# Sums of gate weights added up in DRAM by accumulating DMAs in place of subtractions on VectorE

## The chip, the cores and the metric

One core of a Trainium2 chip runs the whole program. The metric is device time in microseconds: three runs of the kernel before took 1419.89, 1419.94 and 1420.02 us, so the median is 1419.94 us. Everything is float32. Products on TensorE are made from operands split into a high part (fp32r) and a low remainder, so that each product is three matmuls (high by high, high by low, low by high).

## The reference

The input is 1024 tokens by 1024 channels. One wide projection of the normalised input feeds two branches and their gates; the part that the change touches is the gates.

```python
xn = rmsnorm(x, norm1_g[layer])
u = xn @ w_in[layer].astype(f32)
...
q_sb, k_sb, v_sb, f_raw, i_hg, q_hg, g_hg, gate_sb, gate_hg = jnp.split(u, list(c), axis=-1)
...
o_sb = stick_breaking_attention(split_heads(q_sb, SB_HEADS), split_heads(k_sb, SB_HEADS),
                                split_heads(v_sb, SB_HEADS))
...
o_hg = hgrn2_chunkwise(split_heads(jax.nn.silu(q_hg), HG_HEADS), split_heads(k_hg, HG_HEADS),
                       split_heads(i_hg, HG_HEADS), split_heads(log_f, HG_HEADS))
...
o_hg = merge_heads(o_hg) * jax.nn.silu(g_hg)
...
g_a = jax.nn.sigmoid(gate_sb + bg[:D_MODEL])
g_b = jax.nn.sigmoid(gate_hg + bg[D_MODEL:])
merged = g_a * (o_sb @ w_o_sb[layer].astype(f32)) + g_b * (o_hg @ w_o_hg[layer].astype(f32))
h = x.astype(f32) + merged @ w_out[layer].astype(f32)
hn = rmsnorm(h, norm2_g[layer])
a = jnp.square(jax.nn.relu(hn @ w_ff1[layer].astype(f32)))
h = h + a @ w_ff2[layer].astype(f32)
```

## The kernel before

**Stages.** Norm and first projections (up to about 95 us of the profile), attention over 8 heads and 8 query blocks each (64 items, up to about 330 us), the gated recurrence for 4 heads with the first gate products and the attention's output projection as filler (up to about 590 us), the rest of the gates (up to about 718 us), the output projection (up to about 800 us), the MLP.

**Gates.** The four 512x512 quarters of a gate's product (two halves of the tokens by two gates, each over two halves of the channels) are computed by a Strassen-Winograd scheme with seven products instead of eight. For this each gate column block `cb` needs plain weights and four signed sums of weight quarters. There are ten column blocks: `cb` 0 to 7 hold the two merge gates, `cb` 8 and 9 the recurrence's own gate `g_hg`. Class `RawUnit` (L1333) makes two of the seven products ahead, from plain weights and one sum; class `GatePair` (L1530) makes the others from four sums. Both load the plain 128-column strips of `w_in` and form the sums with `sub` (L1291, a VectorE tensor_tensor), then split them.

**Fill work.** `Stream` `st` holds projection jobs (`proj_jobs`, `raw_job`, `i_job`, `sb_job`, listed from L1512) and puts some of their matmuls between the steps of attention and recurrence. When a job starts, `prefetch` splits the weights of the next job and loads those of the one after, so loads run one or two jobs ahead. `RawUnit.split_t` is done in three parts at steps 4, 6 and 8 of the job before (L548).

**Queues.** Weight loads go out on SyncE's queue (SP) in the order of the code (`load`, L135). Accumulating DMAs, and some stores, go out on GpSimd's queue (POOL), where memsets and small norm operations stand too. A DMA that reads or adds to what an earlier one wrote waits, on its issuing engine, for that one's landing; GpSimd's DMAs use eight completion semaphores in turn, so that each also waits for the landing of the eighth before it. An engine runs its instructions in a fixed order, so whatever stands behind a waiting instruction waits too.

**Around the change.** `out_weight_sums` (L1312) already adds up the sums of the output projection's weights in DRAM (`tw`): 16 plain copies and then 16 additions of 256 KB, one in every second item of attention (L2382). At the end of attention GpSimd sums the two halves of the last head's output in place (`osb`, L911); SyncE then stores it (`od`, L922, called at L2404). Behind that store on SyncE's queue stand the loads of the next weights, `wf3` and `wq3` (L136).

Of the kernel before, what the change touches and what calls it, by code (L numbers as in the profile page):

```python
# [39 lines left out]
def kernel(  # L40
# [462 lines left out]
    class Stream:  # L503
# [36 lines left out]
        def step(self):  # L540

            if self.gen is None:
                if self.pos >= len(self.jobs):
                    return False
                self.steps = 0
                self._start()
            self.steps += 1
            if self.owed_t and self.steps in (4, 6, 8):  # L548
                self.owed_t.split_t(hg_level[0] or turn_lo[0], self.steps // 2 - 1)
                if self.steps == 8:  # L550
                    self.owed_t = None
# [760 lines left out]
    def out_weight_sums():  # L1312
# [3 lines left out]
        for op, ways in ((ALU.bypass, plain), (ALU.add, summed)):  # L1316
            for i, src in ways:
                for r in range(4):
                    rs = slice(r * P, (r + 1) * P)
                    after(nc.gpsimd.dma_start(tw[i][rs], src[rs], accum_op=op), lastsel[0])  # L1320
                    yield

    def gate_bias(which, cb):
        return prm[:, BG + which * KT + cb : BG + which * KT + cb + 1]

# [7 lines left out]
    class RawUnit(Unit):  # L1333


        late = True
        turned = 0

        def __init__(self, cb):
            dmas = [  # L1340
                [(0, P, W_IN[:, gate_cols(w, cb)].rearrange("(k p) c -> p k c", p=P))]
                for w in range(2)
            ]
            super().__init__(f"wga{cb}", dmas)
            if cb < KT:
                self.roomy = (1,)

        def split(self):
            if self.hl is not None:
                return  # L1350
            self.load()
            ra, rb = self.raw
# [3 lines left out]
            hi_lo(h, l, ra)  # L1356
            self.hl = [(h, l)]

        def split_t(self, behind=None, upto=3):
            ra, rb = self.raw  # L1360
            while self.turned < upto:
                self.turned += 1
                if self.turned == 1:
                    after(sub(rb, ra, rb), behind)
                elif self.turned == 2:
                    after(sub(rb[:, 512:], rb[:, 512:], rb[:, 0:512]), behind)
                else:
                    t = slot(f"{self.name}t", F32R)
                    self.hl.append((t[:, 0:512], t[:, 512:]))
                    after(hi_lo(*self.hl[1], rb[:, 512:]), behind)  # L1370

    raw_units = [RawUnit(cb) for cb in range(NG)]

    def raw_job(cb):
        u = raw_units[cb]

        def steps_of(ps, wt, w0, half_, k0, start):
            wh, wl = u.hl[wt]
            for k in range(4):
                c = (w0 + k) * P  # L1380
                xh, xl = xn.mov(k0 + k, half_)
                three(
                    ps, wh[:, c : c + P], wl[:, c : c + P], xh, xl, start and k == 0, k == 3, True
                )
                if k % 2 == 1:
                    yield

        def body():
            p1, p14, g1 = (half(f"{n}_{cb}") for n in ("p1", "p14", "g1"))
            ps, p4 = bank(f"pga{cb}"), bank(f"pgq{cb}")  # L1390
# [12 lines left out]
            hi_behind[0] = None  # L1403
            yield from steps_of(p4, 1, 0, 1, 4, True)
            add(p14, p1, p4)
            if cb == 3 or cb == KT - 1:
                whole_input(1, int(cb == KT - 1))
            nc.gpsimd.dma_start(pd[cb][:, 1, :], p14)
# [27 lines left out]
    def sum_forms():  # L1436


        raw = whole
        def split(m, kp, src):  # L1440
            forms[m, kp] = tuple(slot(f"gs{n}{m}{kp}", F32R) for n in "hl")
            hi_lo(*forms[m, kp], src)

        for j in range(2):
            whole_input(0, j)
        yield from range(WAIT)
        s1, s2 = {}, {}
        for kp in range(2):
            s1[kp] = slot(f"gs1{kp}")
            ins = add(s1[kp], raw[1, 0, kp], raw[1, 1, kp])  # L1450
            if kp == 0:
                after(ins, hg_sum[0])
            yield
        for kp in range(2):
            split(5, kp, s1[kp])
            yield
        for kp in range(2):
            s2[kp] = slot(f"gs2{kp}")
            sub(s2[kp], s1[kp], raw[0, 0, kp])
            yield  # L1460
            split(6, kp, s2[kp])
            yield
        gates_in[0].load()
        gates_in[0].load_sums()
        for kp in range(2):
            s3 = slot(f"gs3{kp}")
            sub(s3, raw[0, 0, kp], raw[1, 0, kp])
            split(7, kp, s3)
            yield
        gates_in[0].split()  # L1470
        for kp in range(2):
            s4 = slot(f"gs4{kp}")
            sub(s4, raw[0, 1, kp], s2[kp])
            split(3, kp, s4)
            yield
        gates_in[1].load()
# [35 lines left out]
    for h in range(1, NHS):  # L1512
        j_qk[h] = proj_jobs([qk_item(h)], xn)
        if h == 2:
            raw_job(KT)
        if h == 4:
            q_job(0)
    f_job(0)
    f_job(1)
    q_job(1)  # L1520
# [9 lines left out]
    class GatePair:  # L1530
# [3 lines left out]
        def load(self):  # L1534
            cb = self.cb
            self.raw = [
                wpool.tile([P, 1024], F32, tag="raw", name=f"wg{cb}r{i}") for i in range(2)
            ]
            for i, s_, which in ((0, 0, 0), (0, 1, 1), (1, 1, 1)):
                load(  # L1540
                    self.raw[i][:, s_ * 512 : (s_ + 1) * 512].rearrange("p (k c) -> p k c", k=4),
                    W_IN[i * 512 : (i + 1) * 512, gate_cols(which, cb)].rearrange(
                        "(k p) c -> p k c", p=P
                    ),
                )
# [18 lines left out]
        def split(self, behind=None):  # L1564
            cb = self.cb
            r0, r1 = self.raw
            s0, s1 = slice(0, 512), slice(512, 1024)
            first = behind if self is gates_in[3] else None
# [93 lines left out]

        def y3(self):
            self.product(3, self.Y, False)
            add(self.u2, self.u2, self.Y)
            self.gate(self.u2, 1)

        def early_half(self):
# [740 lines left out]
    for h in range(NHG + 1):  # L2409
# [4 lines left out]
        while going:  # L2414
            going = False
            for g in (lev, tail):
# [9 lines left out]
            st.finish(max(j_f[h + 1], j_q[h + 1]))  # L2426
    st.finish(j_sb[2])
    for _ in side[0]:
        pass
    gates()  # L2430

# [97 lines left out]
```

## Time and profile before

| what | us |
|---|---|
| median of three runs | 1419.94 |
| span of the profiled execution | 1418.4 |
| what lies around the span, by these two | 1.5 |
| TensorE (PE) busy | 1408.7 |
| VectorE (DVE) busy | 1086.9 |
| ScalarE (ACT) busy | 684.9 |
| GpSimd (POOL) busy | 147.3 |

The page gives each engine's busy time, a picture of the span in 40 slices, the DMA queues, the chain of work that ended last and the costliest groups of instructions. In a timeline's row stand start, duration, engine, line, operation, tiles (out<-in) and, in brackets, how long the engine sat idle before it and what ended that. SPq and ACTq are the sequencers that issue DMAs. "f32 x1" or "x1" at the end counts merged instructions.

### The profile page before, as it was taken

The page shows a single profiled execution, that of the slowest core. Times are in us where ns is not written, and L with a number is a line of the kernel's source. Part 1 is how long each engine was busy: PE and PEld are TensorE (multiplying, and loading weights), DVE is VectorE, ACT ScalarE, POOL GpSimd, SP SyncE. Part 2 cuts the span into 40 slices and gives each one's busy share as a digit, 9 for nine tenths or more (in the row PEclk, how much of TensorE's full clock was granted, in tenths as well). Part 3 has the DMA queues.
Part 4 walks back from the last instruction along what each step waited for, and adds up shares of the span by engine and source line. Part 5 has one row for each costly group of instructions (what it writes and reads, how often), then busy time and mean ns, then how long its engine had stood idle before and what let it go on. Part 6 is the DMA issues. An engine that isn't in the chain of part 4 may idle for free.

```text
span 1418.4 us, 18800 instructions
## 1 busy us (share of the span) xinstructions
PE 1408.7 (99%) x6848; PEld 1183.6 (83%) x6848; DVE 1086.9 (77%) x1493; ACT 684.9 (48%) x1183; POOL 147.3 (10%) x341
## 2 busy tenths in 40 slices
PE   9999999999999999999999999999999999999998
PEld 7888888888888888888888888888888888888886
DVE  7679988988567888887788897676666657668765
ACT  6356676664243554433344764445444443534343
POOL 3012223210011031000000300000000000000042
PEclk9999999999999999999999999999999999999999
DMA  7124445535135685364585514444446974776725
GB/s 238 30 67 127 105 100 98 107 77 157 59 74 171 224 225 178 126 215 156 162 298 193 186 54 169 163 163 143 137 145 239 353 265 149 279 273 238 278 94 188
DMA packets 163173, 237.72 MB, mean 168 GB/s; under 512 B 26332, under 2 KB 93448, under 8 KB 163080
## 3 DMA queue, kind: packets, MB, share of 16 engines
q1 hardware_dynamic: 146056, 190.37, 40.0%
q0 software_dynamic: 11584, 34.61, 10.0%
q10 hardware_dynamic: 5440, 11.54, 2.3%
q8 instruction: 54, 0.88, 0.3%
q14 instruction: 39, 0.32, 0.1%
HBM read 168.32 MB, written 66.06 MB: 165 GB/s over the span
## 4 chain that ended last, share of the span: by engine, by line
PE 98%; DVE 1%; ACT 0%; POOL 0%; DMA 0%; issue 0%; POOLq 0%; SPq 0%; DVEq 0%
PE pm L128 21%; PE pX L128 9%; PE pW L128 6%; PE pY L128 6%; PE pjqk L128 6%; PE pga L128 4%; PE gX L128 4%; PE gY L128 4%; PE pjf L128 3%; PE pjq L128 3%; PE pys L128 3%; PE pji L128 3%; PE pyh L128 3%; PE pjv L128 3%; PE po L128 3%; PE z L128 2%
## 5 line engine op out<-in xcount | busy, mean ns | idle before, releaser
L156 ACT CAST whid<-w 128x1024 fp32r<-128x1024 f32 x30 | 31.6, 1053 | 154.5 <-PE pm L128 87.4
L831 DVE TENSOR_TENSOR_SCAN rm<-rm,bits 128x511 f32<-128x511 f32 (+7 forms) x72 | 87.3, 1219 | 16.4 <-ACT rm L809 16.4
L128 PE MATMUL pm<-wlod,sh 128*128 128x512 f32 x240 | 93.5, 390 | 0.0
L128 PE MATMUL pm<-whid,sl 128*128 128x512 f32 x240 | 93.4, 389 | 0.0
L128 PE MATMUL pm<-whid,sh 128*128 128x512 f32 x240 | 93.4, 389 | 0.0
L128 PE MATMUL pm<-tl,sh 128*128 128x512 f32 (+1 forms) x210 | 81.3, 387 | 0.0
L128 PE MATMUL pm<-th,sl 128*128 128x512 f32 (+1 forms) x210 | 81.3, 387 | 0.0
L128 PE MATMUL pm<-th,sh 128*128 128x512 f32 (+1 forms) x210 | 81.3, 387 | 0.0
L161 DVE TENSOR_TENSOR wlod<-w,whid 128x1024 fp32r<-128x1024 f32 x30 | 36.7, 1222 | 55.3 <-ACT whid L156 55.3
L161 DVE TENSOR_TENSOR sl<-sa,sh 128x1024 fp32r<-128x1024 f32 x56 | 68.2, 1218 | 0.0
L156 ACT CAST wTh<-pw 128x512 fp32r<-128x512 f32 (+2 forms) x96 | 43.8, 485 | 41.9 <-PE pw L131 41.0
L2148 POOL TENSOR_SCALAR fss<-fss 128x1 f32<-128x1 f32 x8 | 4.5, 561 | 562.0 <-ACT fsc L2143 561.5
L156 ACT CAST sh<-sa 128x1024 fp32r<-128x1024 f32 x56 | 57.2, 1046 | 7.2 <-DMA sa<-ad 7.2
L161 DVE TENSOR_TENSOR wTl<-pw,wTh 128x512 fp32r<-128x512 f32 (+2 forms) x96 | 49.9, 546 | 4.6 <-ACT wTh L156 4.4
L128 PEld LDWEIGHTS pm<-wlod,sh 128*128 128x128 f32 x240 | 45.1, 188 | 10.0 <-DVE wlod L161 0.4
L128 PEld LDWEIGHTS pm<-whid,sh 128*128 128x128 f32 x240 | 45.0, 188 | 9.5
L128 PEld LDWEIGHTS pm<-whid,sl 128*128 128x128 f32 x240 | 45.0, 188 | 9.1
L169 DVE TENSOR_TENSOR bt<-bt,rm 128x511 f32<-128x511 f32 (+7 forms) x72 | 48.9, 684 | 3.5
L809 ACT ACTIVATE rm<-z 128x511 f32<-128x511 f32 (+4 forms) x96 | 48.0, 500 | 5.5 <-PE z L128 2.8
L128 PE MATMUL pX<-sqh,t1l 128*128 128x512 f32 x128 | 49.9, 390 | 0.0
L128 PE MATMUL pX<-sql,t1h 128*128 128x512 f32 x128 | 49.9, 390 | 0.0
L128 PE MATMUL pX<-sqh,t1h 128*128 128x512 f32 x128 | 49.8, 389 | 0.0
(932 smaller groups left out, 4434.8 us busy)
## 6 DMA issues: line engine op xcount, KB each, us to landing
w<-in_w_ff_dram SPq DMA_DIRECT2D x72, 512.0 KB, 4.8
sa<-ad SPq DMA_DIRECT2D x52, 512.0 KB, 6.4
ad<-a SPq DMA_DIRECT2D x32, 256.0 KB, 4.3
ad<-s SPq DMA_DIRECT2D x16, 512.0 KB, 3.3
tw<-in_w_out_dram POOLq DMA_DIRECT2D x24, 256.0 KB, 4.6
pr<-pd SPq DMA_DIRECT2D x10, 512.0 KB, 6.0
x<-in_x_dram SPq DMA_DIRECT2D x8, 512.0 KB, 7.8
xnl<-xnh POOLq DMA_DIRECT2D x8, 512.0 KB, 6.5
```

The source lines that it names most:

```text
L128: return pe(nc.tensor.matmul(*a, **k))
L156: hi_last[0] = after(in_turn("act", nc.scalar.copy(dst, src)), hi_behind[0])
L161: nc.vector.tensor_tensor(out=dst, in0=src, in1=hi.bitcast(F32), op=ALU.subtract),
L169: return nc.vector.tensor_tensor(out=out, in0=a, in1=b, op=ALU.mult)
L809: nc.scalar.activation(rm[:, s0 + c0 - 1 : s0 + m - 1], z[:, c0:m], AF.Sigmoid, scale=-0.125)
L831: sc = nc.vector.tensor_tensor_scan(out=rr, data0=rr, data1=bits[:, 1024 - nk + a : 1024 - nk + b][:, ::-1], initial=rm[:, b : b + 1] if i ...
L2148: nc.gpsimd.tensor_scalar(out=ssq, in0=ssq, scalar1=1.0 / D, scalar2=EPS, op0=ALU.mult, op1=ALU.add)
```

## The change

The sums of the gate weights are no longer formed on VectorE. They are added up in DRAM, once and for all columns, into `tg1` to `tg4` (1 and 3 stacked as `tg13`), by 43 DMAs on GpSimd's queue: 32 on blocks of 128 rows by 1024 columns for the merge gates (8 of them copy an earlier sum), and 11 on 512 rows of pairs of 128-column strips for `g_hg` (`gh_sum`), which move runs of 512 bytes. Each moves 512 KB. The 32 DMAs for the output weights follow in the same generator. It is stepped in every second item of attention (32 steps) and at every step of the recurrence (43 steps). The signs of the scheme are turned so that every sum is an addition, and in five places where products or input sums are combined `add` and `sub` change over. `RawUnit` now loads one plain strip and one sum (256 KB instead of 512 KB) and splits the sum in one part; `GatePair` loads three sums and one plain quarter (1 MB instead of 768 KB) and has no subtraction left. The jobs `raw_job(KT)` and `q_job(0)` change places.

```diff
@@ class Stream, step()
-            if self.owed_t and self.steps in (4, 6, 8):
-                self.owed_t.split_t(hg_level[0] or turn_lo[0], self.steps // 2 - 1)
-                if self.steps == 8:
-                    self.owed_t = None
+            if self.owed_t and self.steps == 6:
+                self.owed_t.split_t(hg_level[0] or turn_lo[0])
+                self.owed_t = None
@@ new
+    def gate_weight_sums():
...
+        def add_up(dst, src, op):
+            after(nc.gpsimd.dma_start(dst, src, accum_op=op), lastsel[0])
+
+        def gh_sum(t, *terms):
+            for j, (i, which) in enumerate(terms):
+                add_up(gh_of(tg[t]), gh(i, which), ALU.add if j else ALU.bypass)
+                yield
...
+        def steps(t, op, src):
+            for r in range(4):
+                add_up(part(t, r), part(src, r) if type(src) is int else block(*src, r), op)
+                yield
...
+        yield from both(
+            gh_sum(4, (0, 0), (0, 1), (1, 0), (1, 1)), steps(1, ALU.bypass, (0, 0))
+        )
+        yield from steps(1, ALU.add, (0, 1))
+        yield from steps(2, ALU.bypass, 1)
+        yield from steps(2, ALU.add, (1, 1))
+        yield from steps(4, ALU.bypass, 2)
+        yield from steps(4, ALU.add, (1, 0))
+        yield from steps(3, ALU.bypass, (0, 1))
+        yield from both(gh_sum(2, (0, 0), (0, 1), (1, 1)), steps(3, ALU.add, (1, 1)))
+        outs = out_weight_sums()
+        yield from both(gh_sum(1, (0, 0), (0, 1)), (next(outs) for _ in range(2)))
+        yield from both(gh_sum(3, (0, 1), (1, 1)), (next(outs) for _ in range(2)))
+        yield from outs
...
@@ class RawUnit
-                if self.turned == 1:
-                    after(sub(rb, ra, rb), behind)
-                elif self.turned == 2:
-                    after(sub(rb[:, 512:], rb[:, 512:], rb[:, 0:512]), behind)
...
+            load(t[:, 0:512].rearrange("p (k c) -> p k c", k=4), gate_sum(tg[4], self.cb))
@@ class GatePair, load() and split()
+            load(r0, gate_sum(tg13, cb))
+            load(r1[:, 0:4], gate_sum(tg[2], cb))
+            load(r1[:, 4:8], W_IN[512:, gate_cols(1, cb)].rearrange("(k p) c -> p k c", p=P))
...
-            after(sub(r0[:, s0], r0[:, s1], r0[:, s0]), first)
-            sub(r1[:, s0], r1[:, s1], r0[:, s0])
...
-            sub(r0[:, s1], r1[:, s1], r0[:, s1])
@@ signs
-            ins = add(s1[kp], raw[1, 0, kp], raw[1, 1, kp])
+            ins = sub(s1[kp], raw[1, 0, kp], raw[1, 1, kp])
...
-            self.y_sum = add(p1, p1, self.Y)
-            add(p1, p1, self.X)
+            self.y_sum = sub(p1, self.Y, p1)
+            sub(p1, p1, self.X)
@@ jobs
         if h == 2:
+            q_job(0)
+        if h == 4:
             raw_job(KT)
-        if h == 4:
-            q_job(0)
@@ attention, then recurrence
-    wsums = out_weight_sums()
+    wsums = gate_weight_sums()
...
-        if i % 2 == 1:
+        if i % 2 == 0:
             next(wsums, None)
...
                 if next(g, StopIteration) is not StopIteration:
                     going = True
+                    next(wsums, None)
```

The instruction order on GpSimd's queue, where attention ends and the recurrence begins. `tw` are the sums of the output weights, `pd9` the store of the last product made ahead in attention, `osb7` the summing of the last head's output, `hss0` and `hn0` the first norm of the recurrence. Before:

```order
L867 MEMSET wTh7_2_4_3586 128x128
L867 MEMSET wTl7_2_4_3587 128x128
L1320 DMA tw_131<-tw_131 128x512
L1408 DMA pd9_112<-p14_9_3649 128x512
L911 DMA osb7_3545<-osb7_3545 64x1024
L265 TENSOR_SCALAR hss0_0_4326<-hss0_0_4326 128x4
L269 TENSOR_TENSOR hn0_0_y_4339<-hss0_0_4326,expo_91 128x4
```

The same place now, from the first DMA behind the last memsets of attention; `512x2x128` marks the strips of `gh_sum`, `128x1024` the blocks:

```order
L1336 DMA tg2_143<-in_w_in_dram 512x2x128
L1336 DMA tg13_142<-in_w_in_dram 128x1024 x2
L1336 DMA tg2_143<-in_w_in_dram 512x2x128
L1336 DMA tg13_142<-in_w_in_dram 128x1024 x2
L1336 DMA tg2_143<-in_w_in_dram 512x2x128
L1336 DMA tg13_142<-in_w_in_dram 512x2x128
L1319 DMA tw_131<-in_w_out_dram 128x512
L1465 DMA pd9_112<-p14_9_3649 128x512
L1319 DMA tw_131<-in_w_out_dram 128x512
L1336 DMA tg13_142<-in_w_in_dram 512x2x128 x2
L1319 DMA tw_131<-in_w_out_dram 128x512 x2
L910 DMA osb7_3545<-osb7_3545 64x1024
```

Behind `osb7` follow one more strip DMA, 28 for `tw`, and only then `hss0`. So the 43 steps written into the recurrence stand together on GpSimd's queue, ahead of the recurrence's first norm, and 14 of them stand ahead of `osb7`. The second strip DMA of `tg2` adds to what the first wrote, and the third to the second, so each waits for the landing of the one before it; so does the second strip DMA of `tg1` in `tg13`.

SyncE's queue at the same place. `wir` are the weights of the recurrence's values, `od3` the store of `osb7`, `wf3` and `wq3` the next projections' weights, `wga0` those of the first `RawUnit` of the recurrence. Before:

```order
L136 DMA wir3_3691<-in_w_in_dram 128x2x512
L922 DMA od3_3547<-osb7_3545 64x1024
L136 DMA wf3r0_3743<-in_w_in_dram 128x8x128
L136 DMA wq3r0_4276<-in_w_in_dram 128x8x128
L136 DMA wga0r0_4282<-in_w_in_dram 128x8x128
L136 DMA wga0r1_4284<-in_w_in_dram 128x8x128
```

Now:

```order
L136 DMA wir3_3690<-in_w_in_dram 128x2x512
L921 DMA od3_3547<-osb7_3545 64x1024
L136 DMA wf3r0_3742<-in_w_in_dram 128x8x128
L136 DMA wq3r0_4291<-in_w_in_dram 128x8x128
L136 DMA wga0r0_4297<-in_w_in_dram 128x8x128
L136 DMA wga0r1_4299<-tg4_144 128x4x128
```

Nothing has moved here but the source of `wga0`'s second load: the store of `osb7` still stands ahead of the loads of `wf3` and `wq3`.

More of the change, by code (lines that the diff above doesn't have):

```diff
@@ L1321, in out_weight_sums, with gh, gh_of, block @@
                     yield
+    TGW = NG * P
+    tg13 = dram("tg13", [1024, TGW])
+    tg = {1: tg13[0:512], 3: tg13[512:1024]}
+    tg.update({i: dram(f"tg{i}", [512, TGW]) for i in (2, 4)})
+    def gate_weight_sums():
+        def gh(i, which):
+            rows = W_IN[i * 512 : (i + 1) * 512, C_GH : C_GH + HGW]
+            return rows.rearrange("k (c w p) -> w k c p", w=2, p=P)[which]
+        def gh_of(t):
+            return t[:, KT * P :].rearrange("k (c p) -> k c p", p=P)
+        def add_up(dst, src, op):
[4 more added lines that the diff above has]
+                yield
+        def block(i, which, r):
+            c0 = (C_GA, C_GB)[which]
+            return W_IN[i * 512 + r * P : i * 512 + (r + 1) * P, c0 : c0 + D]
+        def part(t, r):
+            return tg[t][r * P : (r + 1) * P, 0:D]
+        def steps(t, op, src):
+            for r in range(4):
+                add_up(part(t, r), part(src, r) if type(src) is int else block(*src, r), op)
+                yield
+        def both(a, b):
+            for _ in a:
+                yield
+                if next(b, StopIteration) is not StopIteration:
+                    yield
+            yield from b
+        yield from both(
[12 more added lines that the diff above has]
+        yield from outs
+    def gate_sum(t, cb):
+        return t[:, cb * P : (cb + 1) * P].rearrange("(k p) c -> p k c", p=P)
     def gate_bias(which, cb):
@@ L1336, with load @@
         late = True
-        turned = 0
+        turned = False
         def __init__(self, cb):
[L1340 to L1346, printed above, removed]
+            src = W_IN[:, gate_cols(0, cb)].rearrange("(k p) c -> p k c", p=P)
+            super().__init__(f"wga{cb}", [[(0, P, src)]])
+            self.cb = cb
+        def load(self):
+            if self.raw is not None:
+                return
+            super().load()
+            if self.cb < KT:
+                t = slot(f"{self.name}r1")
+            else:
+                t = wpool.tile([P, 1024], F32, tag="raw", name=f"{self.name}r1")
+            load(t[:, 0:512].rearrange("p (k c) -> p k c", k=4), gate_sum(tg[4], self.cb))
+            self.raw.append(t)
         def split(self):
@@ L1351, in split @@
             self.load()
-            ra, rb = self.raw
             h, l = (
@@ L1355, in split, with split_t @@
             )
-            hi_lo(h, l, ra)
+            hi_lo(h, l, self.raw[0])
             self.hl = [(h, l)]
[L1359 to L1362, printed above, removed]
-                if self.turned == 1:
-                    after(sub(rb, ra, rb), behind)
-                elif self.turned == 2:
-                    after(sub(rb[:, 512:], rb[:, 512:], rb[:, 0:512]), behind)
[L1367 to L1370, printed above, removed]
+        def split_t(self, behind=None):
+            if not self.turned:
+                self.turned = True
+                t = slot(f"{self.name}t", F32R)
+                self.hl.append((t[:, 0:512], t[:, 512:]))
+                after(hi_lo(*self.hl[1], self.raw[1][:, 0:512]), behind)
     raw_units = [RawUnit(cb) for cb in range(NG)]
@@ L1389, in body @@
             p1, p14, g1 = (half(f"{n}_{cb}") for n in ("p1", "p14", "g1"))
-            ps, p4 = bank(f"pga{cb}"), bank(f"pgq{cb}")
+            ps, pq = bank(f"pga{cb}"), bank(f"pgq{cb}")
             if 6 <= cb < KT:
@@ L1403, in body @@
             hi_behind[0] = None
-            yield from steps_of(p4, 1, 0, 1, 4, True)
-            add(p14, p1, p4)
+            yield from steps_of(pq, 1, 0, 1, 4, True)
+            add(p14, p1, pq)
             if cb == 3 or cb == KT - 1:
@@ L1472, in sum_forms @@
             s4 = slot(f"gs4{kp}")
-            sub(s4, raw[0, 1, kp], s2[kp])
+            add(s4, raw[0, 1, kp], s2[kp])
             split(3, kp, s4)
@@ L1538, in load @@
             ]
[L1539 to L1545, printed above, removed]
+            r0, r1 = (r.rearrange("p (k c) -> p k c", k=8) for r in self.raw)
+            load(r0, gate_sum(tg13, cb))
+            load(r1[:, 0:4], gate_sum(tg[2], cb))
+            load(r1[:, 4:8], W_IN[512:, gate_cols(1, cb)].rearrange("(k p) c -> p k c", p=P))
             if cb >= KT:
@@ L1567, in split @@
             s0, s1 = slice(0, 512), slice(512, 1024)
-            first = behind if self is gates_in[3] else None
-            after(sub(r0[:, s0], r0[:, s1], r0[:, s0]), first)
-            sub(r1[:, s0], r1[:, s1], r0[:, s0])
             h, l = (
@@ L1664, in y3 @@
             self.product(3, self.Y, False)
-            add(self.u2, self.u2, self.Y)
+            sub(self.u2, self.Y, self.u2)
             self.gate(self.u2, 1)
@@ L2428 @@
     for _ in side[0]:
+        pass
+    for _ in wsums:
         pass
```

## The prediction

> **What bounds the kernel now.** I read the page from the top, then the table of waits, then windows.
>
> ```profile
> span 1418.4 us, 18800 instructions
> PE 1408.7 (99%) x6848; PEld 1183.6 (83%) x6848; DVE 1086.9 (77%) x1493; ACT 684.9 (48%) x1183; POOL 147.3 (10%) x341
> PE 98%; DVE 1%; ACT 0%; POOL 0%; DMA 0%; issue 0%; POOLq 0%; SPq 0%; DVEq 0%
> ```
>
> TensorE is busy for all but 9.7 us, and 98% of the chain that ended last is PE. A busy PE is not PE at its peak, so I looked at what PE waits for (total, times, longest), and at how many matmuls it gets through in stages of different kinds (columns: window, its length, then busy time and count of PE, PEld, DVE, ACT, POOL, then clock, DMA share, GB/s).
>
> ```profile
> PE warm L128 <- POOL ident masks.py:199: 2.2, 1, 2.2
> PE po L128 <- DVE wTl L161: 0.3, 1, 0.3
> 600.00:700.00 100.00, 100.00 (x443) 82.81 (x442) 82.67 (x120) 32.53 (x44) 8.13 (x15) 1.00 0.54 174
> 1000.00:1100.00 100.00, 100.00 (x443) 82.81 (x442) 68.49 (x96) 46.37 (x67) 0.00 (x0) 1.00 0.51 180
> ```
>
> The largest wait is 2.2 us at the start; after it the largest is 0.3. The gate stage (600 to 700), where the subtractions stand, runs 443 matmuls per 100 us, the MLP (1000 to 1100) the same 443, both at granted clock 1.00, although VectorE is busy 82.67 us in the one and 68.49 in the other. So no wait on VectorE hides in the matmul rate, and PE has no idle time in which a late operand could be made good: what PE once waits is lost in full.
>
> **What goes.** Each `RawUnit` had two subtractions, each `GatePair` three; ten of each make 50.
>
> ```profile
> L1292 DVE TENSOR_TENSOR wga7r<-wga7r,wga7r 128x1024 f32<-128x1024 f32 x1 | 1.2, 1233 | 0.0
> L1292 DVE TENSOR_TENSOR wg3r<-wg3r,wg3r 128x512 f32<-128x512 f32 x2 | 1.4, 690 | 0.0
> ```
>
> One of the five is 1024 wide, four 512: 10 x 1.23 + 40 x 0.69 = 39.9 us of VectorE. PE's instructions are the same in kind and number, so their saving is worth what PE waits for VectorE: 0.3 us, as above. I take 0. The turned signs swap `add` for `sub` on one shape, 0. The parts of `split_t` merged into one: same work, 0. The two swapped jobs have the same matmuls, 0.
>
> **Loads.** A `GatePair` loads 256 KB more, a `RawUnit` 256 KB less. Ten times 256 KB over the gate stage (about 590 to 718 us) are 2.6 MB in 128 us, 20 GB/s on top of 174, with DMA engines 0.54 busy: hidden. Were that cover gone, 256 KB would cost a unit what its load lasts, 5.0 us in the row of `wg0` below. The first DMAs for `g_hg` stand ahead of attention's first copies of q on POOL's queue. One issue costs 0.53 us in a plain row, and 1.05 us in an adding one (rows below); the far end for a strip DMA with its runs of 512 bytes, which the trace does not show on this queue, is eight times that, 8.4 us.
>
> ```profile
> 91.00 0.53 POOL L698 DMA_DIRECT2D QL<-QL  x1 [0.71 <-DVE QL L161]
> 99.87 0.39 PE L128 MATMUL z<-KS,QL 128*128 128x512 f32 x1
> QL<-QL POOLq DMA_DIRECT2D x16, 128.0 KB, 2.2
> L1433 POOL DMA_DIRECT2D xnl<-xnh x8 | 7.5, 1047 | 5.7 <-PE pjq L128 4.8 <-PE pga L128 0.8
> wg0r<-in_w_in_dram SPq DMA_DIRECT2D x3, 256.0 KB, 5.0
> ```
>
> (The third row and the last are groups of DMA issues: KB each, us from issue to landing; so are those further on. The fourth is a group of instructions: busy, mean ns of one, idle before.) The copy lands at 93.2 and is read at 99.87: 6.7 us of room, so the far end costs 1.7 us, the near one nothing; I take 0.
>
> **The DMAs added.** 32 of 75 are stepped through attention, one per two items (about 7 us apart), so they keep up. But the order of POOL's queue shows that the 43 written into the recurrence stand in one block right behind attention's last memsets, 14 of them ahead of `osb7`, the sum of the last head's output. The block starts where today's last addition for `tw` is issued, at 306.9.
>
> ```profile
> 306.88 0.81 POOL L1320 DMA_DIRECT2D tw<-tw  x1
> 323.19 0.59 POOL L1408 DMA_DIRECT2D pd<-p  x1 [15.50 <-DVE p L1289]
> 328.16 0.85 POOL L911 DMA_DIRECT2D osb<-osb  x1 [4.38 <-ACT osb L907]
> 333.61 0.51 SPq L922 DMA_DIRECT2D od<-osb  x1
> 336.36 0.37 SPq L136 DMA_DIRECT2D wf3r<-in_w_in_dram  x1
> 340.23 1.05 ACT L156 CAST wf3h<-wf3r 128x1024 fp32r<-128x1024 f32 x1 [0.55 <-DMA wf3r<-in_w_in_dram]
> 343.53 0.62 ACT L1067 COPY ksl<-k 128x512 f32<-128x512 f32 x1
> 346.60 0.60 PE L128 MATMUL sl<-q,ksl 128*128 128x128 f32 x4
> ```
>
> Read from the bottom: PE's `sl` at 346.60 needs ACT's copy `ksl`, done at 344.15, so 2.45 us of room. On ACT that copy stands behind the CAST of `wf3`, which starts when its load has landed, 3.87 us after the issue (340.23 - 336.36). That load stands on SP's queue behind the store `od`, which waits until `osb` has landed (`od` is issued at 333.61, so at about 333.5). If `osb` lands late, the CAST starts 0.1 + 0.51 + 3.87 = 4.5 us after the landing, and PE stalls for landing + 4.5 - 340.23 - 2.45 = **landing - 338.2**. Today's room is 4.7 us. Behind the waiting `od` stand the loads of `wf3`, `wq3` and `wga0`, behind the CAST all of ACT's work.
>
> When does `osb` land? Each adding DMA on strips waits, at issue, for the one before it on the same sums, and each DMA for the landing of the eighth before it, so POOL cannot run far ahead of the landings. Two stretches show accumulations alone on POOL's queue (one `osb` with two and three `tw` sums).
>
> ```profile
> 266.90:274.60 7.70, 7.70 (x42) 6.44 (x41) 6.24 (x11) 5.02 (x12) 2.35 (x10) 1.00 0.77 103
> 298.20:306.90 8.70, 8.70 (x55) 7.74 (x55) 7.96 (x12) 4.48 (x13) 3.59 (x16) 1.00 0.82 122
> xnl<-xnh POOLq DMA_DIRECT2D x8, 512.0 KB, 6.5
> hd<-h POOLq DMA_DIRECT2D x8, 512.0 KB, 3.3
> GB/s 238 30 67 127 105 100 98 107 77 157 59 74 171 224 225 178 126 215 156 162 298 193 186 54 169 163 163 143 137 145 239 353 265 149 279 273 238 278 94 188
> ```
>
> They moved 103 and 122 GB/s with the DMA engines 0.77 and 0.82 busy, mean 112; 512 KB accumulated land in 6.5 us, 512 KB stored plainly in 3.3. Ahead of `osb`, with itself, stand four block additions, two of the three strip DMAs of `tg2` and one of `tg1`, which all add: 7 x 0.524 + 0.262 = 3.93 MB, at 112 GB/s 35 us. So the additions alone end at 306.9 + 35 = **342**. Plain traffic in the same time: three strip copies, one block copy (the last step that attention takes), four of `tw`, the `pd` store, four loads `wir` and some ACT stores, about 6 MB; at 353 GB/s, the highest slice of the page, 17 us. Were nothing of it hidden, `osb` would land at **359**. The windows leave a fifth of the DMA time free, 7 of 35 us; that hides 7 of the 17, and the other 10 come on top: 306.9 + 35 + 10 = **352**. The stall is 352 - 338.2 = 13.8 us, the ends 3.8 and 20.8.
>
> Later on the queue stand 29 more DMAs ahead of the recurrence's first norm. By the same prices (17 additions, 4.7 MB, 42 us; 12 plain, 3.1 MB, 9 us) they end at 352 + 51 = 403.
>
> ```profile
> 403.84 0.19 POOL L265 TENSOR_SCALAR hss<-hss 128x4 f32<-128x4 f32 x1 [74.83 <-ACT hon L1247]
> L136 SPq DMA_DIRECT2D wout2r<-tw x2: 377/377/377, 712.6 to 715.4; - x2
> wir<-in_w_in_dram SPq DMA_DIRECT2D x4, 512.0 KB, 3.9
> wga0r<-in_w_in_dram SPq DMA_DIRECT2D x2, 512.0 KB, 4.6
> ```
>
> That norm stands at 403.84 today and moves back with the stall to 417, so 14 us of room: 0. The first `tw` block is read at 712.6: 0.
>
> **Sum.** Span 1418.4 + 13.8 = 1432.2, and the 1.5 us by which the median (1419.94) is above this execution's span give **1433.7 us**. Its own range: 1419.9 + 3.8 = 1423.7 to 1419.9 + 20.8 = 1440.7. The strips' short runs are a term that I left at the blocks' price: loads in runs of 512 bytes (`wga0`, 4.6 us) last 1.2 times those in longer runs (`wir`, 3.9), so three adding strips (14 us) would cost 2.8 more: 1443.5, which I round up to 1445.
>
> **Rivals.**
> (1) *The queue keeps up.* If additions move like plain stores, the 10 MB ahead of and with `osb` take 28 us at 353 GB/s, end at 335, under 338.2, and nothing stalls: 1419.9 (within 0.2%, or 2.8 us, about what a measurement of this kernel can tell from no change). For it: the additions in the two windows never had more than four in a row, so their queue may not have been full. Against it: `xnl`, 512 KB in 6.5 us. Chance 0.20.
> The Trainium skill bears on this rival ("DMA: Bandwidth & Descriptors", section "Anatomy of one DMA — SWDGE (gpsimd) path"): it fits a GpSimd DMA by some 2.0 us and its bytes over 436 GB/s, without a word on accumulation. By that, an estimate, 512 KB would land in 3.2 us; the trace agrees for the plain `hd` (3.3) and not for the accumulating `xnl` (6.5). By the fit the 3.93 MB of additions would take 9 us behind a full queue, and the sum would be 1419.9.
> (2) *The strips are much dearer.* If runs of 512 bytes make an addition four times as slow, three of them cost 3 x 14 us more, and the time is about 1475. For it: an accumulation reads and writes each run, and no row shows one on short runs. Against it: the 1.2 of the loads. Chance of over 1445: 0.10.
> (3) *Faster: VectorE's relief in attention.* Two `RawUnit`s are split there, in a stretch where VectorE is busy 92%:
>
> ```profile
> 100.00:200.00 100.00, 100.00 (x577) 86.46 (x576) 91.52 (x127) 69.86 (x158) 23.29 (x86) 1.00 0.48 114
> ```
>
> Their subtractions, 2 x (1.23 + 0.69) = 3.8 us, would pass to PE if VectorE set the pace there: 1416.1. It decides if PE's instructions last longer for VectorE's sake without a wait in the records. Against it: PE is busy 100.00 of 100, and of PE's waits only 0.3 us name `wTl`. It also needs a block that stalls nothing. Chance 0.03.
>
> **How the numbers follow.** The forecast has 0.67, rival (2) 0.10, both slower by over 0.2%: 0.77. Rival (1) is the 0.20 within 0.2%, rival (3) the 0.03 faster. The range takes in rival (1) and the strips' bound, 1419 to 1445, and leaves out (2) and (3), 0.13.
>
> **What would show it.** In the changed kernel's waits of PE a new row for `sl` of some 14 us near 347, released by ACT's `ksl`, whose chain goes back to the CAST of `wf3`, its load, `od` and `osb`; on SP's queue `od` at about 352 instead of 333.61; POOL's `osb` issued at 345 to 350; nothing new from 600 on. If `od` is issued before 338, rival (1) holds. If the strip DMAs of `tg2` land far over 6.5 us after issue, it is (2). If PE waits somewhere else, above all before 306 or behind 400, my step of the queue's order was wrong: a stall in attention for the first 32 DMAs, or `hss0` late behind the 28 for `tw`.

## The result, and the profile after

The changed kernel takes 1459.86 us (median of four runs, 1458.12 to 1460.68) against 1419.91 for the kernel before: ratio 1.028, 95% interval 1.0265 to 1.0295. It is 40 us slower. The direction is the one forecast, but the size is three times the 13.8 us forecast, and it lies outside the range, which ended at 1445.

The first lines of the changed kernel's page, and the shares of the chain that ended last:

```profile
span 1456.3 us, 18801 instructions
PE 1413.7 (97%) x6848; PEld 1186.7 (81%) x6848; DVE 1054.3 (72%) x1443; ACT 683.8 (47%) x1183; POOL 187.9 (13%) x384
PE 92%; DMA 3%; DVE 2%; issue 1%; ACT 1%; POOL 1%; POOLq 0%; SPq 0%; ACTq 0%; DVEq 0%
```

The span is 37.9 us longer. PE's time outside its busy time went from 9.7 to 42.6 us (1456.3 - 1413.7), so 32.9 us are waits; the other 5.0 are in PE's busy time, although its instructions are the same. The chain, once 98% PE, now runs through DMAs for 3% of the span. What PE waits for (total, times, longest):

```profile
PE sl L128 <- ACT ksl L1066: 25.5, 1, 25.5
PE sd L128 <- ACT sd_h L156: 5.3, 2, 4.8
PE warm L128 <- POOL ident masks.py:199: 2.2, 1, 2.2
PE po L128 <- DVE wTl L161: 0.9, 1, 0.9
```

Two new waits make the loss. The large one is at the `sl` that the prediction named. The other, at `sd`, was not forecast. Windows of the gate stage and of the MLP, as before (columns as in the prediction):

```profile
600.00:700.00 100.00, 100.00 (x443) 82.81 (x442) 71.99 (x100) 35.09 (x48) 6.47 (x12) 1.00 0.56 181
1000.00:1100.00 100.00, 100.00 (x443) 82.81 (x442) 69.44 (x96) 46.88 (x67) 0.00 (x0) 1.00 0.43 150
```

VectorE has fallen from 82.67 to 71.99 us in 100, and PE still runs 443 matmuls: nothing gained and nothing lost there. The place of the loss, from the timelines of GpSimd, SyncE, ScalarE and PE, in order of the chain:

```profile
312.21 22.70 SPq L136 DMA_DIRECT2D wir<-in_w_in_dram  x4
332.22 1.04 ACT L156 CAST wih<-wir 128x1024 fp32r<-128x1024 f32 x1 [8.49 <-DMA tg<-in_w_in_dram]
336.48 0.79 PE L128 MATMUL sd<-sd_h,ones 128*128 128x512 f32 x1 [4.75 <-ACT sd_h L156]
342.82 1.95 POOL L910 DMA_DIRECT2D osb<-osb  x1
351.61 0.51 SPq L921 DMA_DIRECT2D od<-osb  x1
351.72 1.05 PE L128 MATMUL sl<-q,ksl 128*128 128x128 f32 x8
352.29 0.46 SPq L136 DMA_DIRECT2D wf3r<-in_w_in_dram  x1
352.84 1.22 SPq L136 DMA_DIRECT2D wq3r<-in_w_in_dram  x1
370.45 1.04 ACT L156 CAST wf3h<-wf3r 128x1024 fp32r<-128x1024 f32 x1 [20.67 <-DMA wf3r<-in_w_in_dram]
380.78 1.04 ACT L156 CAST wq3h<-wq3r 128x1024 fp32r<-128x1024 f32 x1 [9.29 <-DMA wq3r<-in_w_in_dram]
382.40 2.08 PE L128 MATMUL sl<-q,ksl 128*128 128x128 f32 x8 [25.54 <-ACT ksl L1066]
441.09 0.19 POOL L265 TENSOR_SCALAR hss<-hss 128x4 f32<-128x4 f32 x1 [49.29 <-ACT hon L1246]
```

`od` went out at 351.61 (forecast: about 352), so the last head's sum landed when it was expected to. But the loads behind it did not take 3.87 us: `wf3` was split 18.2 us after its issue (370.45 - 352.29) and `wq3` 27.9 us after (380.78 - 352.84). The first row and the second show the same earlier: the second of the four `wir` loads reaches ScalarE at 332.22, where it did at 324.19 before. (The bracket of that row names a `tg` DMA, which this CAST does not read; that the load of `wir` ended the wait is inferred from what the CAST reads.) The recurrence's first norm (441.09) still waits for ScalarE, not for the 28 sums ahead of it. The DMA queues from 352.2 to 380.8 (q0 is GpSimd's, q1 SyncE's; share of 16 engines' time; then KB and us to landing), and two rows of the same view from 308 to 351.6:

```profile
q0 software_dynamic: 3087, 5.67, 89.9%
q1 hardware_dynamic: 2160, 1.31, 17.3%
wq3r<-in_w_in_dram SPq DMA_DIRECT2D x1, 512.0 KB, 27.9
...
tg<-in_w_in_dram POOLq DMA_DIRECT2D x12, 512.0 KB, 9.5
wir<-in_w_in_dram SPq DMA_DIRECT2D x4, 512.0 KB, 10.1
```

The DMA engines were full, nine tenths of it with sums, and SyncE's queue needed 2160 packets for 1.31 MB, most of them 512 bytes long. In the kernel before, the `sl` ahead of the one that now waits, and the load of `wq3` (DMA view from 307 to 340), were:

```profile
341.61 1.05 PE L128 MATMUL sl<-q,ksl 128*128 128x128 f32 x8
wq3r<-in_w_in_dram SPq DMA_DIRECT2D x1, 512.0 KB, 5.1
```

### The profile page after: what moved, and what is told of

The parts are those of the page before. It is cut to its first block, busy times and chain, and to the rows that moved or that the text cites. A ratio compares the mean times of both kernels' runs of the same rounds, so it can differ in the third digit from the quotient of the medians.

```text
span 1456.3 us, 18801 instructions
## 1 busy us (share of the span) xinstructions
PE 1413.7 (97%) x6848; PEld 1186.7 (81%) x6848; DVE 1054.3 (72%) x1443; ACT 683.8 (47%) x1183; POOL 187.9 (13%) x384
## 4 chain that ended last, share of the span: by engine, by line
PE 92%; DMA 3%; DVE 2%; issue 1%; ACT 1%; POOL 1%; POOLq 0%; SPq 0%; ACTq 0%; DVEq 0%
PE pm L128 21%; PE pX L128 9%; PE pW L128 6%; PE pY L128 6%; PE pjqk L128 5%; PE gX L128 4%; PE gY L128 4%; PE pga L128 3%; PE pys L128 3%; PE pyh L128 3%; PE pjv L128 3%; PE pjq L128 3%; PE pji L128 3%; PE pjf L128 2%; PE po L128 2%; PE pwX L128 2%
## 5 line engine op out<-in xcount | busy, mean ns | idle before, releaser
L156 ACT CAST wTh<-pw 128x128 fp32r<-128x128 f32 (+3 forms) x96 | 44.0, 486 | 42.7 <-PE pw L131 39.0
L128 PE MATMUL sl<-q,ksl 128*128 128x128 f32 x192 | 26.6, 282 | 25.5 <-ACT ksl L1066 25.5
```

Of the source, the lines that this page charges most:

```text
L128: return pe(nc.tensor.matmul(*a, **k))
L156: hi_last[0] = after(in_turn("act", nc.scalar.copy(dst, src)), hi_behind[0])
```

## The experiments

Three theories stood against each other: (1) the loads meet the queue of sums and are slowed by it; (2) only the order on SyncE's queue matters (a store that waits, loads behind it), as the prediction had it; (3) the extra DMA traffic costs its time wherever it stands. Times are medians; the kernel before was measured beside them at 1419.97 to 1420.07.

**Without the late sums.** The 43 DMAs are left out; the loads that would read their sums take plain weights of the same shape.

```diff
-                    next(wsums, None)
...
-    for _ in wsums:
-        pass
...
-            load(r0, gate_sum(tg13, cb))
+            load(r0, W_IN[:, gate_cols(0, cb)].rearrange("(k p) c -> p k c", p=P))
```

> The 43 sums that stand behind attention are left out; the loads that would read them take plain weight columns of the same shape, so the gates and the output projection are computed from wrong weights. All else of the change stays: 32 sums in attention, no subtractions, turned signs, swapped jobs. If the loss comes from the block of 43 alone, as I think: the waits near 336 and 382 are gone, and what is left is the 0.5 us that the trace of the change shows at 167, so 1420.4 us (1419.5 to 1421). If a part of the loss comes from the other edits (the 32 sums in attention, the larger loads of the gate stage), it stays here: 1423 or more. If VectorE's relief were worth something that the block hid, under 1417.

Measured: 1421.42 us, ratio 1.0011 (1.0001 to 1.002). That is a little over the expected range. Of the 40 us, 38.4 belong to the 43 DMAs. The rest is one wait, in the waits of PE:

```profile
PE po L128 <- DVE wTl L161: 1.8, 1, 1.8
```

**The jobs back in their places**, on top of that; the first products then take a plain strip in place of `tg4`.

```diff
         if h == 2:
-            q_job(0)
+            raw_job(KT)
         if h == 4:
-            raw_job(KT)
+            q_job(0)
```

> As the run without the 43 late sums (1421.42), with the jobs q_job(0) and raw_job(KT) back in their old places; the first products ahead then take a plain weight strip in place of the sum tg4, which would not be ready, so they too are computed from wrong weights. If the 1.5 us left in that run, a wait of PE for wTl near 168, come from the swapped jobs: 1419.9 to 1420.3. If they come from the 32 sums in attention or the loads: 1421 to 1422 still.

Measured: 1420.18 us, ratio 1.0001 (0.9992 to 1.001), and the row above is back at 0.3 us. So the remaining 1.2 us come with the swapped jobs (or with `tg4` as their source, which changed in the same step), and the rest of the change, the 50 subtractions and the 32 sums in attention among it, moves nothing.

**The store on GpSimd's queue.**

```diff
-    keep_attended(nc.sync)
+    keep_attended(nc.gpsimd)
```

> The store of the last head's sum is issued by GpSimd in place of SyncE, so the loads of wf3 and wq3 no longer stand behind a store that waits; the block stays whole. Theory 1 (the loads take turns, packet by packet, with the queue of sums): the loads are issued near 345, but meet the sums and still take 15 to 28 us, the first wait (near 336, 9.8 us with what follows) stays and the second shrinks from 25.5 to 10 to 20 us: 1440 to 1452 us. Theory 2 (the order on SyncE's queue alone, as I predicted): the second wait is gone, 1431 us.

Measured: 1436.26 us, ratio 1.0118 (1.0101 to 1.0134). SyncE's and ScalarE's timelines and PE's waits:

```profile
344.49 0.37 SPq L136 DMA_DIRECT2D wf3r<-in_w_in_dram  x1
353.68 1.06 ACT L156 CAST wf3h<-wf3r 128x1024 fp32r<-128x1024 f32 x1 [3.42 <-DMA wf3r<-in_w_in_dram]
...
PE sd L128 <- ACT sd_h L156: 5.9, 2, 5.3
```

The time lies between the two expectations. The second wait is gone, as theory 2 said, and the first is as it was; a new one of 1.5 us, on a DMA, stands at `pkv`. But the load still took 9.2 us (353.68 - 344.49), over twice its time before: it was through before most of the `tw` sums were issued. This run alone does not decide between (1) and (2).

**29 sums held back** behind the recurrence's norms (`norm_seen` is set after each of them); the others stay.

```diff
+            norm_seen[0] = last_power[0]
...
-            after(nc.gpsimd.dma_start(dst, src, accum_op=op), lastsel[0])
+            after(after(nc.gpsimd.dma_start(dst, src, accum_op=op), lastsel[0]), norm_seen[0])
...
+    for _ in range(14):
+        next(wsums, None)
```

> The 14 sums ahead of the last head's sum stay where they are, the other 29 are held back behind the recurrence's norms (most after 440 us). The store still waits on SyncE's queue until 351. Theory 1: wf3 and wq3 now land 4 to 6 us after issue, not 18 and 28, so PE's second wait is 3 to 5 us and the first stays: 1433 to 1437 us. Theory 2 (the late store is the whole cause of the second wait): nothing changes there, about 1458. If the later sums are as dear wherever they stand (theory 3), a new wait appears after 440 and the time stays over 1445.

Measured: 1448.82 us, ratio 1.0202 (1.0187 to 1.0217). ScalarE's timeline and PE's waits:

```profile
360.44 1.04 ACT L156 CAST wf3h<-wf3r 128x1024 fp32r<-128x1024 f32 x1 [10.11 <-DMA wf3r<-in_w_in_dram]
362.58 1.04 ACT L156 CAST wq3h<-wq3r 128x1024 fp32r<-128x1024 f32 x1 [1.10 <-DMA wq3r<-in_w_in_dram]
...
PE sl L128 <- ACT ksl L1067: 8.3, 2, 6.8
```

The loads were issued at the same time as in the changed kernel (352.35 and 352.90), and are there after 8.1 and 9.7 us in place of 18.2 and 27.9, with one sum of strips beside them in place of that and 28 of `tw`. The wait falls from 25.5 to 6.8 us. That is theory 1; theory 2 would have left it. The total missed its expectation (1433 to 1437), because the 29 sums cost again where they were put: PE's instructions run 19.9 us late against the kernel before where that is at 349 us, and 28.5 us late at the last one.

**All 43 spread** behind the norms (the same edit without the loop over 14).

> All 43 sums are issued behind the recurrence's norms, one a step from the first norm on (about 404 to 590 us), nothing left out. Theories 1 and 2 (the loss is one of place): both waits gone, 1420 to 1423 us. Theory 3 (22 MB more DMA cost what they cost wherever they stand): over 1435, with new waits of PE for gate weights between 410 and 600. A gain below 1417 would mean that the relief of VectorE is worth something after all.

Measured: 1431.75 us, ratio 1.0087 (1.0072 to 1.0102), between the two expectations. PE's waits:

```profile
PE gX L128 <- DVE gu L1290: 2.9, 1, 2.9
...
PE pga L128 <- ACT p L1458: 1.8, 1, 1.8
PE po L128 <- DVE wTl L161: 1.7, 1, 1.7
PE pot L131 <- DVE hon L169: 1.5, 1, 1.5
PE sl L128 <- DVE q L169: 0.9, 1, 0.9
```

Both large waits are gone. The one at `po` is that of the run without the late sums; the others are new and stand from 450 us on, among them one at `pot` for a norm that GpSimd makes between the sums. So theory 3 is right by at most 12 us of the 40. Whether these come from the traffic or from GpSimd's order, no run here separates. No placing tried here beats the kernel before, and leaving the sums out altogether does not either.

**29 sums directly behind `osb`**, all of them for `tw` (`last_sum` is the DMA that sums the last head); the other three for `tw` and the 11 of gate weights behind the norms.

```diff
+        yield from out_weight_sums()
         yield from both(gh_sum(2, (0, 0), (0, 1), (1, 1)), steps(3, ALU.add, (1, 1)))
...
+    norm_seen[0] = last_sum[0]
+    for _ in range(29):
+        next(wsums, None)
```

> 29 sums (all of the output weights) stand directly behind the last head's sum in place of ahead of it and behind it, the other 14 (gate weights) behind the recurrence's norms. The sum, its store and the issue of wf3 and wq3 are on time (334 to 338). Theory 2 (the order on the queues alone): no wait before 400, and 1431 to 1434 as in the run that spread all 43. Theory 1 (loads beside the sums): wf3 and wq3 take 15 to 28 us from issue, and PE waits 10 to 20 us at the same place as in the changed kernel: 1442 to 1455.

Measured: 1447.95 us, ratio 1.0192 (1.0176 to 1.0208). SyncE, ScalarE, and PE's waits:

```profile
335.17 0.51 SPq L922 DMA_DIRECT2D od<-osb  x1
337.12 0.38 SPq L136 DMA_DIRECT2D wf3r<-in_w_in_dram  x1
356.14 1.04 ACT L156 CAST wf3h<-wf3r 128x1024 fp32r<-128x1024 f32 x1 [15.79 <-DMA wf3r<-in_w_in_dram]
369.61 1.04 ACT L156 CAST wq3h<-wq3r 128x1024 fp32r<-128x1024 f32 x1 [12.43 <-DMA wq3r<-in_w_in_dram]
...
PE sl L128 <- ACT ksl L1067: 23.8, 1, 23.8
```

The store and both issues are on time, within 2 us of the kernel before, and PE waits 23.8 us all the same, since the loads take 19.0 and 31.4 us. No wait at `sd` is left: with no sums ahead of `osb`, `wir` came in time. Theory 2 falls here.

**The block copies in place of adding.** `late` is set where attention ends.

```diff
-            after(nc.gpsimd.dma_start(dst, src, accum_op=op), lastsel[0])
+            after(nc.gpsimd.dma_start(dst, src, accum_op=ALU.bypass if late[0] else op), lastsel[0])
```

> The 43 DMAs of the block copy in place of adding (the sums are then wrong: 25 of them lose their added part), same order, same bytes. If addition in DRAM is what makes the block dear, as my price of 112 GB/s for it said, the last head's sum lands near 340 in place of 351, the loads behind meet half the traffic, and the time is 1425 to 1440 us. If the packets set the price (the trace of the change has the strip copies in packets of 512 bytes at 122 GB/s, all else in longer ones at over 200), copying gains nothing ahead of the last head's sum, whose strip additions become strip copies: it lands at 351 to 358, and the time is 1455 to 1468.

Measured: 1449.18 us, ratio 1.021 (1.0196 to 1.0224), between both expectations. SyncE's timeline and PE's waits:

```profile
345.74 0.52 SPq L921 DMA_DIRECT2D od<-osb  x1
...
PE sl L128 <- ACT ksl L1066: 22.5, 1, 22.5
```

From the block's first DMA to `od` it is 34.9 us here (from 310.8) and 43.6 in the changed kernel (from 308.0). Copying saves a fifth of the block, not half, and the loads behind it are as slow. GpSimd's queue in the changed kernel from 308 to 351.6, and here from 310.8 to 345.8 (packets, MB, share):

```profile
q0 software_dynamic: 4752, 7.34, 82.1%
...
q0 software_dynamic: 2064, 7.34, 67.4%
```

The bytes are the same. The 2688 packets fewer are what three strip DMAs save when they go out in packets of 4 KB in place of 512 bytes (3 x 1024 - 3 x 128). So the strips that add went in short packets and the strips that copy in long ones; the expectation above, which gives the short ones to the copies, has it the wrong way round. Part of what copying saves is therefore in the strips, and this run does not tell it from the part in the blocks.

**Whole-row loads** of `wf3` and `wq3`: 4 KB a run in place of 512 bytes, from other rows of the weights, once in the changed kernel, once with the 29 sums directly behind `osb`.

```diff
+            src = mat[:, c0 : c0 + n].rearrange("(k p) c -> p k c", p=P)
+            if name in ("wf3", "wq3"):
+                src = mat[0:P, c0 - 896 : c0 + 128].rearrange("p (k c) -> p k c", k=8)
```

> The changed kernel, in which the loads of wf3 and wq3 take whole rows of 4 KB (the first 128 rows of the weights) in place of strips with runs of 512 bytes: as many bytes into the same tiles, the same order on every queue; those two projections are computed from wrong weights. Theory 1 as the runs so far sharpen it: on each DMA engine the loads' packets take turns with the sums', one for one. Each load then has 8 packets an engine in place of 64, and wf3 and wq3 land some 4 to 7 us after issue in place of 18.2 and 27.9; PE's second wait falls from 25.5 to 2 to 5 us, the first (4.8) stays, and the time is 1433 to 1438 us. If the queues share by bytes, or the loads wait behind what the sums have in flight, the two still need 18 to 28 us and the time stays at 1455 to 1460.

> The run with 29 sums directly behind the last head's sum (1447.95), with the same whole-row loads of wf3 and wq3 (wrong weights for those two projections). There the two loads were issued on time and landed 19 and 31 us later. Turns one for one: they land 4 to 7 us after issue, PE's wait of 23.8 us falls under 3, and the time is 1421 to 1426. Sharing by bytes: 1445 to 1450 as before.

Measured: 1442.31 us (ratio 1.0158, 1.014 to 1.0177) and 1426.17 us (1.0039, 1.0028 to 1.0051). The first is 4 us above its expectation and the second 0.2; both are far from the rival's. The DMA queues of the first from 352.6 to 363.4, its wait, and that of the second:

```profile
q1 hardware_dynamic: 368, 1.31, 31.3%
wq3r<-in_w_in_dram SPq DMA_DIRECT2D x1, 512.0 KB, 10.1
...
PE sl L128 <- ACT ksl L1069: 7.4, 1, 7.4
...
PE sl L128 <- ACT ksl L1070: 2.7, 1, 2.7
```

The same 1.31 MB of SyncE's queue now are 368 packets, not 2160, and `wq3` lands in 10.1 us in place of 27.9. PE's wait falls from 25.5 to 7.4 us, and in the second run from 23.8 to 2.7.

**Short packets for the sums of the output weights.**

```diff
+                    d, s = (t[rs].rearrange("p (a c) -> a p c", a=4) for t in (tw[i], src))
+                    after(nc.gpsimd.dma_start(d, s, accum_op=op), lastsel[0])
```

> Each DMA of the sums for the output weights goes over its rows in four passes of 512 bytes a row in place of one of 2 KB: same bytes, shorter packets, nothing else moved. Theory 1 (the 128 packets that each DMA engine has for wf3 and wq3 take turns with one packet of the sums each: 27.9 us / 128 = 218 ns a turn): with short packets a turn is some 100 to 120 ns, wq3 lands 13 to 16 us after issue, PE's second wait falls from 25.5 to 10 to 14 us, and the time is 1444 to 1450 although the sums themselves last longer. If loads and sums share by bytes, or wait for one another whole: wq3 lands no earlier than 28 us after issue, 1459 or more.

Measured: 1468.88 us, ratio 1.0344 (1.033 to 1.0359). The run does not test what it was made for: the edit also moved GpSimd's order, so that `osb` was issued at 336.02 and most `tw` sums fell behind the norms, and the loads met other traffic. What it shows is a third place to lose time, in PE's waits:

```profile
PE pot L131 <- DVE hon L169: 25.2, 6, 10.9
```

At `pot` PE waits for norms that GpSimd makes between such sums, once for 10.9 us; that the sums hold the norms up is likely, but not tested by itself.

## Why the prediction was wrong, point by point

- *PE is saturated, VectorE's relief is worth nothing*: right. Without the late sums and with the jobs in their places the time is 1420.18 us against 1419.98, although 50 subtractions are gone. The larger loads of the gate stage are hidden, as said.
- *The 43 sums stand in one block, 14 ahead of `osb`, and the store then holds up SyncE's queue*: right. `od` at 351.61 (forecast 352), and with the store on another queue the second wait is gone.
- *The price of the sums* (additions 35 us, plain traffic 17, 7 of it hidden): the total was right and its parts were not. Copying in place of adding saves 8.7 us of the block where my prices would have saved some 24 (3.93 MB at 353 in place of 112 GB/s are 11 us, not 35). So additions are cheaper than I took them for, and the plain traffic dearer; that the two errors cancelled, and `od` came out at 352, was luck.
- *Rival (2), dearer strips*: right in kind, but not the cause. The first adding strip of `tg2` was issued at 316.33, and the next, which waits for its landing, at 327.87: 11.5 us, over the 6.5 named as the sign, with two block DMAs on the queue beside it. The adding strips did go out in packets of 512 bytes. But `od` was no later than forecast, so this is not what took the time past the range.
- ***"The CAST starts 0.1 + 0.51 + 3.87 = 4.5 us after the landing"*: this step failed.** The 3.87 us were read in a stretch without sums, and used for a load that would run beside 29 of them. Measured: 18.2 us for `wf3`, and `wq3`, which I had not followed further, became the end of the chain with 27.9. With the `tw` sums held back the same loads took 8.1 and 9.7 us, and the wait was 6.8. The size of the miss is that of `wq3`: it took 22.8 us longer than before (27.9 against 5.1), the `sl` behind it came 35.8 us late (382.40 against 346.60), and the difference, 13.0, is close to the 13.8 forecast. I asked what loads do to the sums, and not what the sums do to the loads.
- *The same step, earlier*: the four `wir` loads were counted as plain traffic that slows the sums. That they themselves land late (10.1 us in place of 3.9) was not asked, and it is the wait at `sd`. With the slow stretch behind it, it made PE 10.1 us late (the `sl` at 351.72 against 341.61). By the sum above, an estimate, that cost nothing further here, since PE would have waited as long for the loads. The wait is there in each run with the additions ahead of `osb` (0.8 us where they copy), and in none of those with the sums behind it.
- *A stall costs its length*: too low. PE's busy time grew by 5.0 us, as the last section shows.
- *The queue behind*: right. The norm at 441.09 did not wait for the sums, since the stall moved it too. In the runs that put sums behind it, it was the next thing to suffer.
- *The swapped jobs, 0*: 1.2 us, with `tg4` as their source.

Of the loss in the changed kernel's profile, 37.9 us, the two waits at `sl` and `sd` are 30.8 (25.5 + 5.3) and PE's slower work behind them 5.0; that leaves 2.1, of which 0.6 are the longer wait at `po`, some 1 lies behind PE's last matmul (which starts 36.9 us later, 1448.51 against 1411.66, where the span is 37.9 longer), and the rest is short waits. The two conditions of the large wait were tried one by one: the store off the queue takes it away, since the loads then run ahead of the `tw` sums; the `tw` sums away take most of it; the store on time with the `tw` sums in front of the loads leaves 23.8.

What stays open: the rule by which a DMA engine chooses between queues. One packet of each in turn would give 223 ns a turn for `wf3` and `wq3` (28.5 us over 128 packets an engine), but the window of 352.2 to 380.8 shows 3087 packets of GpSimd's queue beside 2160 of SyncE's, and the whole-row loads needed 8 to 10 us where such turns would give 4 to 7. That loads of the same bytes beside the sums are faster as whole rows is shown; the exact rule is not, and the whole rows also lie elsewhere in memory, which was not separated from their fewer packets. The Trainium skill has a rule for this ("DMA: Bandwidth & Descriptors", section "Queues, rings and completion order"): each engine goes round between the queues for which it has work, a whole packet of several descriptors at a time. The runs fit queues that take turns and a load that pays for many pieces (27.9 us in 512-byte packets, 10.1 as whole rows); how many pieces make a turn no run here shows. The prediction weighed the Trainium skill's fit for a single DMA, and not this rule, which bears on the step that failed.

## What to carry to other kernels

A transfer that is hidden on its own queue is still traffic for every other queue: ask what loads run beside it, in how many packets, and how many microseconds before its use each was issued, and do not price a load by a quiet stretch. Steps written one by one into a loop are spread only if something in the program holds each back; look at the order on the queue that the steps end up on. And taking work from an engine for which nobody waits buys nothing, while its replacement may stand in front of something that is waited for.

## What the runs showed of the hardware

PE's granted clock drops after a wait. Windows of the changed kernel behind the first wait and behind the second (length, then PE's busy time and count, further as above; the clock is the third number from the end):

```profile
340.50:343.50 3.00, 3.00 (x8) 2.32 (x8) 2.91 (x6) 0.78 (x2) 3.00 (x5) 0.50 0.55 113
343.50:346.50 3.00, 3.00 (x13) 2.40 (x13) 2.49 (x3) 1.46 (x2) 1.27 (x2) 0.87 1.38 211
...
382.40:384.50 2.10, 2.10 (x9) 2.10 (x10) 2.10 (x3) 1.10 (x2) 0.00 (x0) 0.50 1.08 196
387.50:390.00 2.50, 2.50 (x17) 2.22 (x16) 0.07 (x1) 1.12 (x2) 1.41 (x3) 1.00 1.07 238
```

After a wait of only 4.75 us PE works at half clock until about 344, some 7.5 us after it resumed at 336.48; after 25.5 us of waiting, until about 385, under 3 us. The shorter wait was followed by the longer slow stretch, which had two more waits of 0.5 and 0.3 us in it. Together they cost the 5.0 us by which PE's busy time grew. The Trainium skill ("TensorE: Matmul & The Clock Gate", Part 1 on the clock gate) says that the clock halves after an idle window of about 3.4 us and comes back after about as much sustained work. The second wait agrees with that; the 7.5 us after the first are longer than it says, perhaps because of the two short waits, which no run here separates. Other runs show the clock fall after shorter waits than the Trainium skill names: in the run with all 43 spread it was 0.52 from 480 to 482, behind the 1.8 us at `pga`, and in the last run with whole rows 0.50 from 353 to 355, behind the 2.7 us at `sl`. With no wait over 2.9 us, PE's busy time in the former still grew by 4.4 us (1413.1 against 1408.7).
